# Expert-gate one-hots in 2-byte form, with the third part of the gate multiplied on ScalarE

## The chip, the cores and the metric

The kernel runs on one core of a Trainium2 chip. The metric is the device time of one execution in microseconds (us); lower is better. A core has TensorE (PE, matrix products; PEld is its weight load), VectorE (DVE), ScalarE (ACT), GpSimd (POOL) and SyncE (SP, which here only issues transfers). Each of these works through its own queue in the order of the program and waits on semaphores for the others.

## The reference, cut to what matters

One transformer layer on 512 tokens of width 1024: a token mixer (differential attention and a spatial gating branch), then a channel mixer that retrieves single-neuron experts by product keys. The change touches only the second part:

```python
def peer(h, w_query, sub_keys, u_tab, v_tab):
    q = rmsnorm((xt @ w_query).reshape(T, PEER_HEADS, 2, PEER_PK_DIM))
    s = jnp.einsum('thpd,pnd->thpn', q, sub_keys).astype(jnp.float32)
    s1, i1 = lax.top_k(s[:, :, 0], PEER_TOPK)
    s2, i2 = lax.top_k(s[:, :, 1], PEER_TOPK)
    cand = (s1[..., :, None] + s2[..., None, :]).reshape(T, PEER_HEADS, n_cand)
    cidx = (i1[..., :, None] * PEER_N_KEYS + i2[..., None, :]).reshape(T, PEER_HEADS, n_cand)
    best, pos = lax.top_k(cand, PEER_TOPK)
    eidx = jnp.take_along_axis(cidx, pos, axis=-1)
    gate = jax.nn.softmax(best, axis=-1)
    ...
        act = jax.nn.gelu(jnp.einsum('td,thkd->thk', xb, u_tab[ib]), approximate=False) * gb.astype(xb.dtype)
        return jnp.einsum('thk,thkd->td', act, v_tab[ib])
```

There are 8 heads, 16 picks a head (128 picks a token) and 128 x 128 = 16,384 experts; all data is fp32.

## The kernel before

Tokens come in four tiles of 128. For three of them (NB = 3, tiles 0 to 2) no expert is gathered. The kernel computes the activation of every expert for all 384 tokens, block by block (128 blocks of 128 experts), and multiplies it by a dense gate matrix that is zero except at a token's picks. The fourth tile (NA = 1) is done by gathering: 128 steps, each fetches one picked row of u and v for each token (1 MB, `fetch`, issued by POOL), takes the dot product on DVE (`dot`, tile `dj`), then GELU and the gate, and adds the scaled v row to `acc` on DVE (`accumulate`).

The stretches that matter here, in order:

1. Query products and scores (PE), with the first U blocks between them. A U block (`u_pass`, `next_u`) is 24 matrix products of 384 columns for 128 experts (three products, high and low halves, for each of 8 slices), then a GELU on ACT (tile `gS`) and a spill to DRAM (`gS_d`). The fp32 weights of a block are split by `w_split`: ACT writes `w_hi` (line 173) and DVE writes `w_lo` = raw minus `w_hi` (line 184). The split that a U block issues is that of the block two further on.
2. `merge` (lines 899 to 959), all on DVE but one exponential: the top 16 of the candidates of a head (`top16`, eight times a tile), the place of each pick in the two lists, and the two key numbers of each pick by a one-hot sum over 16 (tile `eq`, in fp32: compare, multiply, reduce, four halves a tile). It is a generator. `advance(x)` runs it piece by piece until the pieces' declared costs (the numbers that it yields) have used up x. Tiles 3 and 0 come before the gate loop, tiles 1 and 2 inside it.
3. The gate loop (from line 1115): 48 batches of 8 tokens. For each token the 128 x 128 gate matrix is a product over the 128 picks of two one-hot matrices: `oh_a` (which second key; on ACT as relu(1 - (iota - key)^2), two batches ahead) and `oh_b` (which first key, times the gate; on DVE, one batch ahead). `gate_matrix` multiplies them on PE in fp32 (line 1106, tile `ps_G`), ACT evicts to `stg` (line 1108), and every second batch 1 MB goes to `G_d`. After each batch stand one U block (`next_u`), a piece of `merge` (`advance(2.8)`) and, from batch 10, gather steps up to a planned share (`gather_to`; PICKS_G is the share that is due by batch 42).
4. U blocks that are left over, then the V stage: 128 blocks, each loads `gS` and, every eighth block, a slab `Gc` of the gate matrix, multiplies them (`at`), splits (`ah`, `al`) and accumulates 18 products of 512 columns in `po`. From block 74 a U block comes with each. PICKS_V is the share of gather steps between V blocks 4 and 74.

PE, DVE, ACT and POOL run in the order in which the code is written; only SP's transfers are ordered by the framework. At most three splits (`w_hi`, `w_lo`) are alive, and four raw blocks.

## Time and profile before

| | |
|---|---|
| device time, median of 3 runs | 2055.9 us (2055.06 to 2058.75) |
| the profiled execution, its own time | 2058.6 us |
| its span, first to last instruction | 2056.8 us |
| mean granted TensorE clock | 0.983 of full |
| busy: PE, DVE, ACT, POOL | 1929.4, 1607.0, 1008.4, 389.8 us |
| bytes moved, mean rate | 484.40 MB, 236 GB/s |

A busy sum over the whole span hides that the stages differ: in the V stage PE has no gap, in the gate loop all three of PE, DVE and ACT are busy for most of the time. So it is read by stretch, and in the gate loop by the start of each batch on PE.

### The profile page before, as it was taken

The numbers are of one execution on the slowest core, as the hardware profiler recorded it, in microseconds if no ns is written. First come the engines' busy times: TensorE is split into PE (matmuls) and PEld (weight loads), VectorE is DVE, ScalarE is ACT, GpSimd is POOL, SyncE is SP. The second block draws the span as 40 slices with busy tenths as digits, with TensorE's granted clock in tenths as the row PEclk, the third lists the DMA queues.
The fourth block names the chain that finished last, engine by engine and source line by source line (L and its number), as shares of the span: only waits on it lengthen the run. The fifth ranks groups of instructions, "written<-read, shape, count | busy, mean of one in ns | idle before, by whom it ended". The sixth has DMA issues, their size and how long they took to land.

```text
span 2056.8 us, 28318 instructions
## 1 busy us (share of the span) xinstructions
PE 1929.4 (94%) x10042; PEld 1693.9 (82%) x10042; DVE 1607.0 (78%) x3108; ACT 1008.4 (49%) x1947; POOL 389.8 (19%) x237
## 2 busy tenths in 40 slices
PE   6989999999989899789889999899999999999997
PEld 5768888887868798688888999688888899998996
DVE  7657877736775657999998785688888899899887
ACT  4235555544433455446889987333333333333333
POOL 0023232101000124330002110011112133333321
PEclk9999999999989999999999999999999999999999
DMA  8753323244875454346659999899998799989982
GB/s 320 276 165 88 94 77 103 79 158 125 277 237 200 137 158 154 120 164 207 190 182 322 306 320 294 302 320 335 324 332 315 273 346 353 341 324 344 347 313 96
DMA packets 171229, 484.40 MB, mean 236 GB/s; under 512 B 14384, under 2 KB 82896, under 8 KB 152528
## 3 DMA queue, kind: packets, MB, share of 16 engines
q1 hardware_dynamic: 152656, 348.37, 50.5%
q0 software_dynamic: 18432, 134.23, 17.8%
q8 instruction: 79, 1.29, 0.2%
q14 instruction: 62, 0.51, 0.1%
HBM read 424.72 MB, written 49.43 MB: 231 GB/s over the span
## 4 chain that ended last, share of the span: by engine, by line
PE 64%; DVE 18%; issue 8%; DMA 5%; ACT 4%; POOL 1%; SPq 0%; DVEq 0%; ACTq 0%; POOLq 0%
PE po L202 8%; PE po L203 8%; PE po L204 8%; PE ps_u L204 5%; PE ps_u L203 5%; PE ps_u L202 5%; DVE w_lo L184 2%; PE ps_proj L202 2%; PE ps_G L1106 2%; PE ps_proj L203 2%; PE ps_proj L204 2%; DMA w_raw<-in_wada 2%; PE ps_s L488 2%; ACT oh_a L1086 2%; PE ps_o L522 2%
## 5 line engine op out<-in xcount | busy, mean ns | idle before, releaser
L173 ACT ACTIVATE w_hi<-w_raw 128x1024 fp32r<-128x1024 f32 x370 | 391.1, 1058 | 466.8 <-issue 269.1
L184 DVE TENSOR_TENSOR w_lo<-w_raw,w_hi 128x1024 fp32r<-128x1024 f32 x330 | 404.6, 1227 | 170.9 <-ACT w_hi L173 166.1
L838 POOL DMA_INDIRECT uv<-in_uv,eidx x128 | 211.2, 1650 | 872.5 <-DVE acc L854 534.9
L204 PE MATMUL ps_u<-h2B,w_lo 128*128 128x384 f32 x1024 | 348.1, 340 | 18.7 <-DVE w_lo L184 18.7
L202 PE MATMUL ps_u<-h2B,w_hi 128*128 128x384 f32 x1024 | 351.9, 344 | 1.1 <-ACT h2B L770 1.1
L203 PE MATMUL ps_u<-h2B,w_hi 128*128 128x384 f32 x1024 | 347.0, 339 | 0.6 <-DVE r L84 0.6
L202 PE MATMUL po<-w_hi,ah 128*128 128x512 f32 x768 | 304.0, 396 | 7.7 <-ACT ah L1179 7.7
L204 PE MATMUL po<-w_hi,al 128*128 128x512 f32 x768 | 303.9, 396 | 0.0
L203 PE MATMUL po<-w_lo,ah 128*128 128x512 f32 x768 | 303.9, 396 | 0.0
L204 PEld LDWEIGHTS ps_u<-h2B,w_lo 128*128 128x128 f32 x1024 | 194.4, 190 | 21.3 <-DVE w_lo L184 21.3
L202 PEld LDWEIGHTS ps_u<-h2B,w_hi 128*128 128x128 f32 x1024 | 194.7, 190 | 4.3 <-ACT h2B L770 1.5
L203 PEld LDWEIGHTS ps_u<-h2B,w_hi 128*128 128x128 f32 x1024 | 194.4, 190 | 3.8 <-DVE r L84 1.0
L202 PEld LDWEIGHTS po<-w_hi,ah 128*128 128x128 f32 x768 | 144.5, 188 | 40.8 <-ACT ah L1179 8.0
L204 PEld LDWEIGHTS po<-w_hi,al 128*128 128x128 f32 x768 | 144.4, 188 | 35.2
L203 PEld LDWEIGHTS po<-w_lo,ah 128*128 128x128 f32 x768 | 144.4, 188 | 33.0 <-DVE w_lo L184 0.4
L854 DVE SCALAR_TENSOR_TENSOR acc<-uv,act,acc 128x1024 f32<-128x1024 f32 x127 | 163.2, 1285 | 4.5
L845 DVE SCALAR_TENSOR_TENSOR dj<-uv,h2A 128x1024 bf16<-128x1024 f32 x128 | 156.0, 1219 | 0.9
L184 POOL TENSOR_TENSOR w_lo<-w_raw,w_hi 128x1024 fp32r<-128x1024 f32 x40 | 97.3, 2436 | 249.9 <-ACT w_hi L173 245.9
L1177 DVE TENSOR_TENSOR at<-gS,Gc 128x384 f32<-128x384 f32 x128 | 121.2, 947 | 12.3 <-DMA gS<-gS_d 12.3
L1179 ACT ACTIVATE ah<-at 128x384 fp32r<-128x384 f32 x128 | 66.4, 518 | 125.4 <-DVE at L1177 125.1
L812 ACT ACTIVATE gS<-ps_u 128x384 f32<-128x384 f32 x128 | 62.7, 490 | 131.5 <-PE ps_u L204 130.9
L1106 PE MATMUL ps_G<-oh_b,oh_a 128*128 128x128 f32 x768 | 99.8, 283 | 26.2 <-DVE oh_b L1095 25.8
(307 smaller groups left out, 3495.2 us busy)
## 6 DMA issues: line engine op xcount, KB each, us to landing
w_raw<-in_uT SPq DMA_DIRECT2D x128, 512.0 KB, 5.7
w_raw<-in_uv SPq DMA_DIRECT2D x128, 512.0 KB, 6.5
w_raw<-in_w SPq DMA_DIRECT2D x120, 512.0 KB, 3.6
G_d<-stg SPq DMA_DIRECT2D x24, 1024.0 KB, 6.1
Gc<-G_d SPq DMA_DIRECT2D x16, 1536.0 KB, 9.7
ada_w<-in_wada SPq DMA_DIRECT2D x32, 512.0 KB, 10.0
w_raw<-in_wada SPq DMA_DIRECT2D x32, 512.0 KB, 4.4
gS_d<-gS SPq DMA_DIRECT2D x74, 192.0 KB, 3.9
```

The costliest lines, as they stand in the source:

```text
L173: nc.scalar.activation(hi, r, AF.Copy)
L184: eng.tensor_tensor(lo, r, hi.bitcast(F32), op=ALU.subtract)
L202: nc.tensor.matmul(ps, lh, rh, start=first, stop=False)
L203: nc.tensor.matmul(ps, lh, rl, start=False, stop=False)
L204: nc.tensor.matmul(ps, ll, rh, start=False, stop=last)
L812: nc.scalar.activation(g, ps, AF.Gelu)
L838: nc.gpsimd.indirect_dma_start(out=g, out_offset=None, in_=a["uv"], in_offset=bass.IndirectOffsetOnAxis(ap=eidx[:, t - NB, k:k + 1], axis=0))
L845: nc.vector.scalar_tensor_tensor(junk, g[:, :D], 1.0, h2A[t - NB], op0=ALU.mult, op1=ALU.mult, accum_out=act)
L854: nc.vector.scalar_tensor_tensor(acc[t - NB], g[:, D:], act, acc[t - NB], op0=ALU.mult, op1=ALU.add)
L1106: nc.tensor.matmul(pG[:, i], oa[:, q * 4 + i], ob[:, q * 4 + i], start=True, stop=True)
L1177: nc.vector.tensor_tensor(at, gS.pop(b), Gc[b // GCH][:, :, b % GCH], op=ALU.mult)
L1179: nc.scalar.activation(ah, at, AF.Copy)
```

## The change

Six things change together.

- The one-hot sums of `merge` work in 2-byte elements, on all eight heads at once, and the reduce is replaced by a tree of halving adds. The declared cost of a piece goes from 3.4 (four a tile) to 3.6 (two a tile).
- `oh_a` moves from ACT to DVE, as one 2-byte compare over eight tokens, and is made one batch ahead, not two.
- `oh_b` becomes three 2-byte matrices, one for each of three 2-byte parts of the gate. DVE makes the plain one-hot `oh_e` and the first two products; ACT makes the third (`last_part`, eight instructions, one a token, with the rest of the gate as a per-partition scale). `gate_matrix` sums three 2-byte products for each token in place of one fp32 product.
- The gather step's product by the gate moves from DVE to ACT (`gelus`), and GELU and gate of a step are issued ahead of the next `last_part`, so `accumulate` comes one round later.
- `advance(2.8)` in the gate loop becomes `advance(2.2)`.
- PICKS_G goes from 0.2 to 0.16, PICKS_V from 0.24 to 0.26, and RESERVE from 0 to 2 (the loop stops issuing U blocks when only so many are left).

```diff
@@ -823,15 +823,15 @@
...
-    PICKS_G, PICKS_V = 0.2, 0.24
-    RESERVE = 0
+    PICKS_G, PICKS_V = 0.16, 0.26
+    RESERVE = 2
...
-    coming, pend = [], []
+    coming, dots_, pend = [], [], []
...
@@ -845,22 +845,30 @@
...
+    def gelus():
+
+        while dots_:
+            t, k, g, act = dots_.pop(0)
+            nc.scalar.activation(act, act, AF.Gelu)
+            nc.scalar.activation(act, act, AF.Copy, scale=gate[:, t, k:k + 1])
+            pend.append((t, k, g, act))
+
     def accumulate(t, k, g, act):
-        nc.scalar.activation(act, act, AF.Gelu)
-        nc.vector.tensor_tensor(act, act, gate[:, t, k:k + 1], op=ALU.mult)
         if k == 0:
             nc.vector.tensor_scalar_mul(acc[t - NB], g[:, D:], act)
         else:
             nc.vector.scalar_tensor_tensor(acc[t - NB], g[:, D:], act, acc[t - NB], op0=ALU.mult, op1=ALU.add)
 
-    def gather_end(left=0):
-        while len(pend) > left:
+    def gather_end():
+        gelus()
+        while pend:
             accumulate(*pend.pop(0))
 
     def gather_step():
-        gather_end(1)
+        if len(dots_) + len(pend) > 1:
+            gather_end()
         if len(coming) == LEAD or (coming and not steps):
-            pend.append(dot(*coming.pop(0)))
+            dots_.append(dot(*coming.pop(0)))
         if steps:
             coming.append(fetch(*steps.pop(0)))
 
@@ -874,7 +882,8 @@
...
-        iota16 = iota[:, :TOPK]
+        iota16 = k1.tile([P, TOPK // 2, 2], BF16, name="iota16")
+        nc.vector.tensor_copy(iota16, iota[:, :TOPK].rearrange("p (a b) -> p a b", b=2))
...
@@ -933,20 +942,26 @@
...
-            idxf = k1.tile([P, 16, TOPK], F32, name="idxf")
-            nc.vector.tensor_copy(idxf, idx[t])
+            idxb = k1.tile([P, 16, TOPK], BF16, name="idxb")
+            nc.vector.tensor_copy(idxb, idx[t])
+            ij2 = k1.tile([P, 2, NH * TOPK, 2], BF16, name="ij2")
+            nc.vector.tensor_copy(ij2, ij.rearrange("p s h k -> p s (h k)").unsqueeze(3).to_broadcast([P, 2, NH * TOPK, 2]))
             yield 1.1
             nc.scalar.activation(g, g, AF.Exp)
             for p in range(2):
-                for hh in range(0, NH, 4):
-                    eq = pool.tile([P, 4, TOPK, TOPK], F32, name="eq", bufs=1)
-                    nc.vector.tensor_tensor(eq, ij[:, p, hh:hh + 4].unsqueeze(3).to_broadcast([P, 4, TOPK, TOPK]),
-                                            iota16.unsqueeze(1).unsqueeze(1).to_broadcast([P, 4, TOPK, TOPK]),
-                                            op=ALU.is_equal)
-                    iv = idxf.rearrange("p (h s) k -> p h s k", s=2)[:, hh:hh + 4, p]
-                    nc.vector.tensor_tensor(eq, eq, iv.unsqueeze(2).to_broadcast([P, 4, TOPK, TOPK]), op=ALU.mult)
-                    nc.vector.reduce_sum(ef[:, p, hh:hh + 4], eq, axis=AX.X)
-                    yield 3.4
+                eq = pool.tile([P, NH, TOPK, TOPK], BF16, name="eq", bufs=1)
+                shape = [P, NH * TOPK, TOPK // 2, 2]
+                nc.vector.tensor_tensor(eq.rearrange("p h k (a b) -> p (h k) a b", b=2),
+                                        ij2[:, p].unsqueeze(2).to_broadcast(shape),
+                                        iota16.unsqueeze(1).to_broadcast(shape), op=ALU.is_equal)
+                iv = idxb.rearrange("p (h s) k -> p h s k", s=2)[:, :, p]
+                nc.vector.tensor_tensor(eq, eq, iv.unsqueeze(2).to_broadcast([P, NH, TOPK, TOPK]), op=ALU.mult)
+                w = TOPK // 2
+                while w > 1:
+                    nc.vector.tensor_tensor(eq[:, :, :, :w], eq[:, :, :, :w], eq[:, :, :, w:2 * w], op=ALU.add)
+                    w //= 2
+                nc.vector.tensor_tensor(ef[:, p], eq[:, :, :, 0], eq[:, :, :, 1], op=ALU.add)
+                yield 3.6
                 if p == 0:
                     z = sm.tile([P, NH], F32, name="gz")
                     nc.vector.reduce_sum(z, g, axis=AX.X)
@@ -1060,7 +1075,9 @@
 
         with tc.tile_pool(name="pg", bufs=3, space=PSUM) as pgp, tc.tile_pool(name="k2", bufs=2, side="right") as k2:
             stg = {}
-
+            PAIR = [P, 8, P // 2, 2]
+            iota2 = k2.tile([P, P // 2, 2], BF16, name="iota2", bufs=1)
+            nc.vector.tensor_copy(iota2, iota.rearrange("p (a b) -> p a b", b=2))
             pks, oas, obs = {}, {}, {}
 
             def picks_of(t):
@@ -1073,37 +1090,53 @@
                     for k in range(2):
                         nc.tensor.transpose(pt[:, k], ef[:, k].rearrange("p h k -> p (h k)"), ident)
                     nc.tensor.transpose(pt[:, 2], gate[:, t], ident)
-                    pks[t] = k2.tile([P, 3, P], F32, name="pk")
-                    nc.scalar.activation(pks[t], pt, AF.Copy)
+                    pk = k2.tile([P, 4, P, 2], BF16, name="pk")
+                    nc.scalar.activation(pk[:, 0:3], pt.unsqueeze(3).to_broadcast([P, 3, P, 2]), AF.Copy)
+                    g3 = k2.tile([P, P], F32, name="g_rest")
+                    nc.vector.tensor_tensor(g3, pt[:, 2], pk[:, 2, :, 0], op=ALU.subtract)
+                    nc.vector.tensor_copy(pk[:, 3], g3.unsqueeze(2).to_broadcast([P, P, 2]))
+                    nc.vector.tensor_tensor(g3, g3, pk[:, 3, :, 0], op=ALU.subtract)
+                    pks[t] = pk, g3
                 return pks[t]
 
+            def per_token(pk, k, o):
+                return pk[:, k, o * 8:o * 8 + 8].unsqueeze(2).to_broadcast(PAIR)
+
+            def pairs(x):
+                return x.rearrange("p t (a b) -> p t a b", b=2)
+
             def one_hots_a(t, o):
 
-                pk = picks_of(t)
-                oa = oas[t, o] = k2.tile([P, 8, P], F32, name="oh_a", bufs=3)
+                oa = oas[t, o] = k2.tile([P, 8, P], BF16, name="oh_a")
+                nc.vector.tensor_tensor(pairs(oa), iota2.unsqueeze(1).to_broadcast(PAIR), per_token(picks_of(t)[0], 1, o),
+                                        op=ALU.is_equal)
+
+            def one_hots_b(t, o):
+
+                pk = picks_of(t)[0]
+                eq = k2.tile([P, 8, P], BF16, name="oh_e")
+                nc.vector.tensor_tensor(pairs(eq), iota2.unsqueeze(1).to_broadcast(PAIR), per_token(pk, 0, o),
+                                        op=ALU.is_equal)
+                ob = k2.tile([P, 3, 8, P], BF16, name="oh_b")
+                obs[t, o] = ob, eq
+                for k in range(2):
+                    nc.vector.tensor_tensor(pairs(ob[:, k]), pairs(eq), per_token(pk, 2 + k, o), op=ALU.mult)
+
+            def last_part(t, o):
+                ob, eq = obs[t, o]
                 for i in range(8):
-                    k = o * 8 + i
-                    nc.scalar.activation(oa[:, i], iota, AF.Square, scale=-1.0, bias=pk[:, 1, k:k + 1])
-                nc.scalar.activation(oa, oa, AF.Relu, scale=-1.0, bias=ones[:, 0:1])
-
-            def one_hots_b(t, o):
-
-                t0 = o * 8
-                pk = picks_of(t)
-                ob = obs[t, o] = k2.tile([P, 8, P], F32, name="oh_b")
-                for i in range(8):
-                    nc.vector.tensor_scalar(ob[:, i], iota, pk[:, 0, t0 + i:t0 + i + 1], pk[:, 2, t0 + i:t0 + i + 1],
-                                            op0=ALU.is_equal, op1=ALU.mult)
+                    nc.scalar.activation(ob[:, 2, i], eq[:, i], AF.Copy, scale=picks_of(t)[1][:, o * 8 + i:o * 8 + i + 1])
 
             def gate_matrix(t, o):
 
-                oa, ob = oas.pop((t, o)), obs.pop((t, o))
+                oa, (ob, _) = oas.pop((t, o)), obs.pop((t, o))
...
                 for q in range(2):
                     pG = pgp.tile([P, 4, P], F32, name="ps_G")
                     for i in range(4):
-                        nc.tensor.matmul(pG[:, i], oa[:, q * 4 + i], ob[:, q * 4 + i], start=True, stop=True)
+                        for k in range(3):
+                            nc.tensor.matmul(pG[:, i], oa[:, q * 4 + i], ob[:, k, q * 4 + i], start=k == 0, stop=k == 2)
...
@@ -1119,19 +1152,21 @@
             for _ in range(UA):
                 next_u()
             one_hots_a(*batches[0])
+            one_hots_b(*batches[0])
+            last_part(*batches[0])
             for _ in range(UB):
                 next_u()
-            one_hots_a(*batches[1])
-            one_hots_b(*batches[0])
             for i, (t, o) in enumerate(batches):
                 if i + 1 < len(batches):
+                    one_hots_a(*batches[i + 1])
                     one_hots_b(*batches[i + 1])
                 gate_matrix(t, o)
+                gelus()
+                if i + 1 < len(batches):
+                    last_part(*batches[i + 1])
                 if nu[0] < n_ahead - RESERVE:
                     next_u()
-                if i + 2 < len(batches):
-                    one_hots_a(*batches[i + 2])
-                advance(2.8)
+                advance(2.2)
                 gather_end()
                 if i >= G_FROM:
                     gather_to(PICKS_G * (i + 1 - G_FROM) / (G_TO - G_FROM) if i < G_TO else 0)
@@ -1208,6 +1243,7 @@
             else:
                 v_w = w_get("v", b)
             ah, al = parts
+            gelus()
             nxt = None
             if b + 1 < NBLK:
                 if (b + 1) % GCH == 0:
```

ACT's queue through one batch with a gather step and on to the next batch's one-hots, before and then changed. `stg` is the eviction of a batch, `act` the GELU (and gate) of a gather step, `w_hi` the split of the U block two further on, `gS` the GELU of the current U block.

```order
L1108 ACTIVATE stg_10406<-ps_G_10480 128x4x16x8
L1108 ACTIVATE stg_10406<-ps_G_10486 128x4x16x8
L173 ACTIVATE w_hi_10495<-w_raw_10419 128x1024
L812 ACTIVATE gS_10524<-ps_u_10499 128x384
L1086 ACTIVATE oh_a_10527<-iota_5718,pk_9435 128x128 x8
L1087 ACTIVATE oh_a_10527<-oh_a_10527,ones_77 128x1024
L849 ACTIVATE act_10466<-act_10466 128x1
```

```order
L1141 ACTIVATE stg_10680<-ps_G_10766 128x4x16x8
L1141 ACTIVATE stg_10680<-ps_G_10780 128x4x16x8
L852 ACTIVATE act_10754<-act_10754 128x1
L853 ACTIVATE act_10754<-act_10754,gate_5333 128x1
L1128 ACTIVATE oh_b_10763<-oh_e_10761,g_rest_9592 128x128 x8
L173 ACTIVATE w_hi_10807<-w_raw_10719 128x1024
```

The split `w_hi` stood directly behind the eviction; now the eight instructions of the third gate part stand ahead of it, and they read `oh_e`, which DVE writes.

DVE's queue over the same piece of the program, before and then changed. `acc` and `dj` are the accumulation and the dot product of the gather steps.

```order
L1095 TENSOR_SCALAR oh_b_10471<-iota_5718,pk_9435 128x128 x8
L184 TENSOR_TENSOR w_lo_10496<-w_raw_10419,w_hi_10495 128x1024
L850 TENSOR_TENSOR act_10466<-act_10466,gate_5333 128x1
L854 SCALAR_TENSOR_TENSOR acc0_5712<-uv_10247,act_10466,acc0_5712 128x1024
L1095 TENSOR_SCALAR oh_b_10540<-iota_5718,pk_9435 128x128 x8
```

```order
L1118 TENSOR_TENSOR oh_e_10675<-iota2_7932,pk_9590 128x1024
L1123 TENSOR_TENSOR oh_b_10677<-oh_e_10675,pk_9590 128x1024 x2
L184 TENSOR_TENSOR w_lo_10722<-w_raw_10634,w_hi_10721 128x1024
L860 SCALAR_TENSOR_TENSOR acc0_5712<-uv_10257,act_10668,acc0_5712 128x1024
L845 SCALAR_TENSOR_TENSOR dj_10755,act_10754<-uv_10421,h2A0_5331 128x1024
L1111 TENSOR_TENSOR oh_a_10759<-iota2_7932,pk_9590 128x1024
L1118 TENSOR_TENSOR oh_e_10761<-iota2_7932,pk_9590 128x1024
L1123 TENSOR_TENSOR oh_b_10763<-oh_e_10761,pk_9590 128x1024 x2
```

Between one `oh_e` and the next stands `w_lo`, which reads the `w_hi` that ACT now writes behind its third part; the gather step's two instructions stand between `w_lo` and the next `oh_e`, and its multiplication by the gate is gone from here.

SP's queue from the last write of the gate matrix to the first loads of the V stage, before and then changed (`gS_d` writes are the spills of U blocks).

```order
L1112 DMA G_d_85<-stg_11691 128x16x128
L160 DMA w_raw_11877<-in_uv 128x1024
L1173 DMA Gc_11867<-G_d_85 128x3072
L160 DMA w_raw_11909<-in_uv 128x1024
L160 DMA w_raw_11941<-in_uv 128x1024
L821 DMA gS_11863<-gS_d_84 128x384
```

```order
L1145 DMA G_d_85<-stg_12169 128x16x128
L814 DMA gS_d_84<-gS_12300 128x384
L160 DMA w_raw_12369<-in_uv 128x1024
L1208 DMA Gc_12419<-G_d_85 128x3072
L160 DMA w_raw_12429<-in_uv 128x1024
L160 DMA w_raw_12461<-in_uv 128x1024
L821 DMA gS_12415<-gS_d_84 128x384
```

One more U block's spill now stands behind the last write of the gate matrix: four U blocks are left there, against three. The order on every engine is the same with RESERVE at 0 as at 2; the fourth block is there because the cheaper declared pieces of `merge` end the wait for tile 0 one U block earlier.

## Rows read from the trace of the kernel before

**Rows 1.** Busy time by stretch: us, busy of PE, PEld, DVE, ACT, POOL (instructions), clock, DMA.

```profile
800.00:954.00 154.00, 129.56 (x692) 118.06 (x691) 143.97 (x531) 72.97 (x164) 53.00 (x26) 0.97 0.47 161
954.00:1273.00 319.00, 293.38 (x1905) 286.08 (x1906) 268.86 (x707) 285.80 (x644) 33.38 (x23) 1.00 0.80 259
1273.00:1293.00 20.00, 12.27 (x72) 11.95 (x70) 4.60 (x5) 5.30 (x9) 0.00 (x0) 0.93 0.96 326
1293.00:2045.00 752.00, 751.98 (x3528) 646.17 (x3528) 652.04 (x862) 278.66 (x472) 175.52 (x104) 1.00 0.86 313
```

**Rows 2.** Order of time on PE: first, second-last and last gate batch, one U start.

```profile
954.43 2.19 PE L1106 MATMUL ps_G<-oh_b,oh_a 128*128 128x128 f32 x16 [1.05 <-DVE oh_b L1095]
...
1264.80 1.95 PE L1106 MATMUL ps_G<-oh_b,oh_a 128*128 128x128 f32 x16
...
1266.50 0.42 PE L202 MATMUL ps_u<-h2B,w_hi 128*128 128x384 f32 x1
...
1270.77 1.95 PE L1106 MATMUL ps_G<-oh_b,oh_a 128*128 128x128 f32 x16
```

**Rows 3.** Who waited for whom in the gate loop (945 to 1290): us, times, longest.

```profile
DVE act L850 <- ACT act L849: 27.9, 17, 3.5
...
PE ps_G L1106 <- DVE oh_b L1095: 25.8, 23, 2.0
```

**Rows 4.** Order of time on ACT through one batch: start, us, line, instruction.

```profile
1186.82 0.49 ACT L812 ACTIVATE gS<-ps_u 128x384 f32<-128x384 f32 x1 [1.64 <-PE ps_u L204]
1187.21 2.44 ACT L1086 ACTIVATE oh_a<-iota,pk 128x128 f32<-128x128 f32 x8
...
1190.83 1.06 ACT L1108 ACTIVATE stg<-ps_G 128x512 f32<-128x512 f32 x2
1191.79 1.05 ACT L173 ACTIVATE w_hi<-w_raw 128x1024 fp32r<-128x1024 f32 x1
```

**Rows 5.** Order of time on DVE through the gather step of that batch.

```profile
1191.15 1.28 DVE L854 SCALAR_TENSOR_TENSOR acc<-uv,act,acc 128x1024 f32<-128x1024 f32 x1
1192.35 1.22 DVE L845 SCALAR_TENSOR_TENSOR dj<-uv,h2A 128x1024 bf16<-128x1024 f32 x1
...
1193.49 2.13 DVE L1095 TENSOR_SCALAR oh_b<-iota,pk 128x128 f32<-128x128 f32 x8
```

**Rows 6.** The chain of waits in a batch with three top-16 pieces of merge.

```profile
1014.83 2.04 DVE oh_b L1095 x8
1016.87 1.13 DVE w_lo L184
1022.07 2.04 DVE oh_b L1095 x8
```

**Rows 7.** Order of time on DVE: one half-size one-hot sum and the start of the next.

```profile
928.74 1.22 DVE L943 TENSOR_TENSOR eq<-ij,iota 128x1024 f32<-128x1024 f32 x1
...
932.50 1.23 DVE L943 TENSOR_TENSOR eq<-ij,iota 128x1024 f32<-128x1024 f32 x1
```

**Rows 8.** DVE operations by shape: busy us, mean ns, idle before (third row: 954 to 1067).

```profile
L184 DVE TENSOR_TENSOR w_lo<-w_raw,w_hi 128x1024 fp32r<-128x1024 f32 x330 | 404.6, 1227 | 170.9 <-ACT w_hi L173 166.1 <-DMA wsT<-in_wsT 4.2
...
L278 DVE TENSOR_TENSOR rb<-rb,sq 128x512 f32<-128x512 f32 x7 | 4.8, 692 | 6.7 <-ACT sq L277 6.0
...
L905 DVE TENSOR_TENSOR val<-val,rq 128x256 f32<-128x256 f32 x1 | 0.4, 415 | 0.0
...
L934 DVE TENSOR_TENSOR ij<-ij,t 128x128 f32<-128x128 f32 x4 | 1.2, 292 | 0.1
```

**Rows 9.** Order of time on PE: 256-column products, one weight load each.

```profile
145.22 0.28 PE L203 MATMUL ps_proj<-hcT,w_hi 128*128 128x256 f32 x1
145.34 0.28 PE L204 MATMUL ps_proj<-hcT,w_lo 128*128 128x256 f32 x1
```

**Rows 10.** Who waited for whom ahead of the gate loop (800 to 950).

```profile
PE ps_u L204 <- DVE w_lo L184: 18.7, 8, 6.1
```

**Rows 11.** The chain of waits from the U blocks into the V stage.

```profile
1284.19 7.14 DMA gS<-gS_d
```

## Prediction

> **What bounds the kernel now.** I read the stretches first. In the V stage PE is busy for 751.98 of 752 us, so nothing that the change does to DVE or ACT can shorten it, and a gather step moved into it is hidden there. The room is ahead of it: in the gate loop PE, DVE and ACT are busy for 293, 269 and 286 of 319 us, all three close to the limit; ahead of the loop DVE is (144 of 154); and 7.7 us of PE are idle on the way into the V stage [rows 1]. Then I read the starts of the gate batches on PE. From the first to the last it is 316.3 us for 47 intervals, 6.73 us each, while an undisturbed interval takes 5.97: 1.70 for the gate product and 4.27 for the U block [rows 2]. So 47 x 5.97 = 280.6 us is PE at its pace and 35.7 us is waiting. The waits name the two causes: PE waits for `oh_b` (25.8 us in 23 times), and DVE, which makes it, waits for the GELU of a gather step (27.9 us in 17 times) that stands on ACT behind `oh_a` [rows 3, 4].
>
> **The gate product on PE.** 16 half products of fp32 become 24 products of 2-byte elements with a weight load each. No row shows a 2-byte product. The nearest is the 256-column product: 0.12 us each with its own weight load, 0.107 of it the columns at the 2.4 GHz level, so 0.013 over [rows 9]. For 128 columns that gives 0.053 + 0.013 = 0.067 us, or 1.61 us a batch against 1.70: PE's own pace goes from 5.97 to 5.88, 47 x 0.09 = 4 us. The bounds are 0.053 (columns alone) and 0.107 (no faster than the 1.70 / 16 of an fp32 half): a pace of 5.5 to 6.8. I take 0.067. The Trainium skill speaks against even that little: its page "TensorE: Matmul & The Clock Gate", section "Back-to-back issue gap", puts a stream of weight-load and product pairs at 128 columns at about 81 ns, by which 24 would take an estimated 1.94 us, more than the fp32 product, and PE's pace would be 6.2. As the next part shows, PE is not what sets the pace, so the sum moves by 2 to 3 us between the one and the other.
>
> **The new loop through DVE and ACT.** This is where I expect the time to go. The order shows four steps that wait for one another inside one batch. ACT's third part of the next batch reads `oh_e` of DVE. The split `w_hi` stands on ACT behind that third part (before it stood ahead of the one-hots). DVE's `w_lo` reads `w_hi`. And the next `oh_a` and `oh_e` stand on DVE behind `w_lo` and behind whatever `merge` and gather work has been put between. So each batch must pay for all of it in a row:
> third part: eight ACT instructions of 128 elements with a per-partition operand, as `oh_a` had, 2.44 us less the 0.10 by which ACT overlaps neighbours = 2.34 [rows 4]; `w_hi` 1.05 [rows 4]; `w_lo` 1.13 [rows 6]; `oh_a` and `oh_e`; hand-offs, 0.1 in all.
> The two compares are 2-byte operations of 1024 elements, of which the trace has none. Their ends are 1.23 us, an fp32 operation of 1024 elements at one a cycle, and 0.69, one of 512, if pairs go through together [rows 8]. I take 0.69, because both inputs and the output are laid out in pairs of neighbours and every operand is 2-byte: 0.60 + 0.69 = 1.29 (the first overlaps by 0.09, as `w_lo` does). The Trainium skill's page "VectorE: DVE Perf Modes", section "The perf-mode tier table", gives a two-tensor operation on 2-byte SBUF operands twice the fp32 rate, which is the end that I took; no row here can show it, and at the other end the sum would be 2170 instead of 2096 (below).
> The loop is 2.34 + 1.05 + 1.13 + 1.29 + 0.10 = 5.91 us, just above PE's 5.88, and 47 x 5.91 = 277.8. In itself that is no loss. The loss is that DVE's other work is no longer beside it. DVE has only the first two gate products (1.2 us) to do during the third part and the split (3.39 us), then sits idle for some 2.1 us, and everything else stands between `w_lo` and the next `oh_e` and adds to the interval in full:
> - 13 top-16 searches of `merge` in the loop (three are done ahead of it): three take 7.24 - 2.04 - 1.13 = 4.07 [rows 6], so 13 x 1.36 = 17.6.
> - Four one-hot sums of eight heads: 1.23 + 1.23 + 0.69 + 0.42 + 0.3 + 0.3 by fp32 rows of half as many elements [rows 7, 8], with hand-offs 4.3, against 2 x 3.76 before [rows 7]: 17.2 (at one a cycle 7.2 each, 29).
> - Thirty short instructions of about 0.29 [rows 8] and one tile's candidate adds: 10.
> - 18 dots and 18 accumulations of gather steps (20 steps are started in the loop against 26): 18 x (1.20 + 1.14) [rows 5] = 42.1.
> - Two changes of tile, with three more small DVE instructions behind the transposes: 2.
> Together 277.8 + 17.6 + 17.2 + 10 + 42.1 + 2 = 366.7 against 316.3: **+50.4 us**. The wait of 27.9 us for the GELU is gone indeed (GELU and gate stand ahead of the third part now), and so is the DVE multiplication; what comes in its place costs more. PE then idles up to 4 us in the batches with merge work; should its clock drop there, the U block still ends before the next third part does.
>
> **Ahead of the loop.** Tiles 3 and 0 are merged there: four sums at 7.52 - 4.3 = 3.2 less, minus two copies that make the pairs, is 12 us less DVE work in a stretch in which DVE is busy for 94% and PE waits 18.7 us for `w_lo` [rows 1, 10]. One U block (4.27) also leaves this stretch. The first batch comes between 4.3 us (the U block alone) and 16 us (both) earlier; I take 12, since much of PE's wait there is that DVE work. The U block comes back behind the last batch, +4.3: net **-7.7** (0 to -12).
>
> **Into the V stage.** PE idles 7.7 us there, while the load of `gS`, issued when the second-last U block frees its raw block, takes 7.14 us at a DMA share of 0.96 [rows 1, 11]. One more U block ahead of it lets the slab `Gc` land earlier, so the load competes with less, but its issue is still tied to the U blocks: **-2.5** (0 to -7.7). RESERVE does nothing: the loop never comes down to two blocks. The V stage itself: two gather steps more before block 74 at a DMA share of 0.86, no waiting PE: 0.
>
> **Sum.** The profiled execution took 2058.6 us: 2058.6 + 50.4 - 7.7 - 2.5 = 2098.8. It lies 2.7 us above the median of the runs, so I forecast **2096 us** as the median, slower by 40.
>
> **Rivals.** (1) Faster: DVE and ACT are not tied. It needs a `w_hi` that is ready when DVE comes to `w_lo`, which is so when third part and split take no more than the 1.2 us of the two gate products beside them; at the rows' prices they take 3.39. If they did, DVE would set the pace in the ten batches with merge work (10 x 3.5 + 45 = 80) and PE in the other 37 (218): 298 in place of 316.3, and with the other terms 2056 - 18 - 10 = 2027. For it speaks that the loop before ran with all three engines near their limits and that both named waits vanish; against it the order. 0.12. (2) DVE takes one 2-byte element a cycle: 47 x 1.06 + 4 x 2.9 in the loop and 12 us of the gain ahead of it lost: 2096 + 74 = 2170. For it speaks that the operands repeat rows and elements; 0.06. (3) Weight loads hold the product at 0.107 us: PE's pace is 6.84, which binds only in the eight or so batches without merge or gather work: +7 us, inside my range. (4) The tie is real but part of the gather and merge work slips into DVE's idle time: 2050 to 2070; 0.07.
>
> **Numbers.** My own case, 0.75, spans 2070 to 2118 (loop at 5.75 a batch, all terms at their good ends; or the stretch ahead of the loop giving nothing, with (3)). The range of 8 in 10 is 2060 to 2125; it leaves out (1), (2) and the lower part of (4). About 0.2% (4 us) is what a measurement of this kernel can tell from no change. Slower by more: 0.84; within: 0.03; faster: 0.13.
>
> **What would show it.** Right: batch starts on PE of about 5.9 us in the last batches, 7 to 8.3 with gather steps and 9 to 10 with three searches or a sum; DVE idle in front of `w_lo`, released by `w_hi`, some 2 us a batch and near 100 us in all; `ps_G` released by ACT; `oh_a` at 0.7 us; the V stage still without a gap. Wrong: a loop of 300 us or less with `w_lo` not waiting (then rival 1), or `oh_a` at 1.2 us (rival 2).

## The result, and the profile after

The changed kernel takes **2110.8 us** (median of 4 runs, 2109.4 to 2111.9) against 2056.9 for the kernel before, measured beside it: a ratio of 1.026 (95% interval 1.025 to 1.027). It is slower by 54 us, where 40 was forecast. Its profiled execution took 2111.8 us, with a span of 2109.6.

The view of busy time by stretch, with the stretches cut at the first and last gate batch and at the first product of the V stage (columns as in [rows 1]):

```profile
800.00:954.00 154.00, 132.38 (x678) 120.90 (x676) 140.00 (x574) 68.90 (x159) 53.68 (x27) 0.92 0.47 158
954.00:1320.00 366.00, 295.31 (x2263) 277.55 (x2262) 260.68 (x457) 238.83 (x609) 24.30 (x18) 0.93 0.68 211
1320.00:1345.00 25.00, 18.61 (x122) 18.16 (x122) 7.59 (x8) 10.43 (x20) 0.00 (x0) 0.98 0.86 283
1345.00:2098.00 753.00, 752.89 (x3528) 646.64 (x3528) 650.52 (x772) 307.59 (x587) 175.91 (x109) 1.00 0.88 321
```

The V stage still has no gap, and the stretch ahead of the gate loop is as long as it was. In the loop, 366 us now, PE has the busy time of before, and DVE and ACT have less than before (261 and 239 us, against 269 and 286 in [rows 1]). Each is busy for a smaller share of it, and the loop has become longer. That is how a chain of engines that wait for one another looks.

The starts of the first and last gate batch on PE, in order of time; they answer to [rows 2]:

```profile
954.02 0.23 PE L1139 MATMUL ps_G<-oh_b,oh_a 128*128 128x128 bf16 x1
...
1320.01 0.23 PE L1139 MATMUL ps_G<-oh_b,oh_a 128*128 128x128 bf16 x1
```

The loop's 47 intervals take 366.0 us against 316.3. So the difference of 52.8 us between the two spans is divided as follows: up to the first gate batch -0.4, the loop +49.7, from the last gate batch to the first V product +2.6 (22.2 us before, 24.8 after), the rest +1.0.

The waits of DVE, ACT and PE inside the loop (954 to 1320); they answer to [rows 3]:

```profile
DVE w_lo L184 <- ACT w_hi L173: 101.3, 47, 2.2
...
ACT oh_b L1128 <- DVE oh_e L1118: 99.7, 47, 5.6
ACT act L852 <- DVE dj L845: 26.8, 18, 2.3
...
PE ps_G L1139 <- DVE oh_b L1123: 70.5, 72, 5.7
```

DVE waits for ACT once in each of the 47 intervals, and ACT waits for DVE once in each: they take turns. PE waits for DVE's two gate products, up to twice a batch. The start of a longer batch shows it, on DVE, ACT and PE:

```profile
969.09 1.29 DVE L1123 TENSOR_TENSOR oh_b<-oh_e,pk 128x1024 bf16<-128x1024 bf16 x2
969.14 2.44 ACT L1128 ACTIVATE oh_b<-oh_e,g_rest 128x128 bf16<-128x128 bf16 x8 [5.27 <-DVE oh_e L1118]
969.83 0.29 PE L1139 MATMUL ps_G<-oh_b,oh_a 128*128 128x128 bf16 x1 [3.68 <-DVE oh_b L1123]
970.43 2.61 PE L1139 MATMUL ps_G<-oh_b,oh_a 128*128 128x128 bf16 x23 [0.31 <-DVE oh_b L1123]
972.80 0.67 PE L202 MATMUL ps_u<-h2B,w_hi 128*128 128x384 f32 x1
```

All 72 waits of PE end 0.05 to 0.06 us after a gate product of DVE; ACT's third part has begun before that and does not hold PE up. So the third part costs its time not at PE but in the turns of ACT and DVE. The 27.9 us that DVE waited for the GELU of a gather step are gone, as was intended; in its place ACT waits for the dot product (26.8 us), within its turn.

One turn without merge or gather work, first on DVE, then on ACT, in order of time (start, us):

```profile
1072.65 1.22 DVE L184 TENSOR_TENSOR w_lo<-w_raw,w_hi 128x1024 fp32r<-128x1024 f32 x1 [2.19 <-ACT w_hi L173]
1073.79 0.69 DVE L1111 TENSOR_TENSOR oh_a<-iota,pk 128x1024 bf16<-128x1024 bf16 x1
1074.39 0.68 DVE L1118 TENSOR_TENSOR oh_e<-iota,pk 128x1024 bf16<-128x1024 bf16 x1
1075.11 1.29 DVE L1123 TENSOR_TENSOR oh_b<-oh_e,pk 128x1024 bf16<-128x1024 bf16 x2
1078.60 1.22 DVE L184 TENSOR_TENSOR w_lo<-w_raw,w_hi 128x1024 fp32r<-128x1024 f32 x1 [2.20 <-ACT w_hi L173]
```

```profile
1075.17 2.45 ACT L1128 ACTIVATE oh_b<-oh_e,g_rest 128x128 bf16<-128x128 bf16 x8 [1.22 <-DVE oh_e L1118]
1077.53 1.04 ACT L173 ACTIVATE w_hi<-w_raw 128x1024 fp32r<-128x1024 f32 x1
```

From one `w_lo` to the next it is 5.95 us. Within them `w_lo` ends at 1073.87, `oh_e` at 1075.07, the third part at 1077.62 and `w_hi` at 1078.57; then `w_lo` can start. All that DVE has to do meanwhile is the 1.3 us of the first two gate products.

### The profile page after: what moved, and what is told of

Read it like the earlier page. It is cut to its first block, busy times and chain, and to the rows that moved or that the text cites. A ratio compares the mean times of both kernels' runs of the same rounds, so it can differ in the third digit from the quotient of the medians.

```text
span 2109.6 us, 28649 instructions
## 1 busy us (share of the span) xinstructions
PE 1939.3 (92%) x10426; PEld 1693.4 (80%) x10426; DVE 1594.5 (76%) x2803; ACT 989.7 (47%) x2027; POOL 380.4 (18%) x237
## 4 chain that ended last, share of the span: by engine, by line
PE 55%; DVE 19%; ACT 9%; issue 6%; DMA 4%; POOL 1%; ACTq 0%; POOLq 0%; DVEq 0%
PE po L204 8%; PE po L202 8%; PE po L203 8%; ACT oh_b L1128 5%; PE ps_u L203 4%; PE ps_u L204 4%; PE ps_u L202 4%; DVE w_lo L184 4%; ACT w_hi L173 2%; PE ps_proj L202 2%; DMA w_raw<-in_wada 2%; PE ps_proj L203 2%; PE ps_proj L204 2%; PE ps_s L488 2%; PE ps_o L522 1%
## 5 line engine op out<-in xcount | busy, mean ns | idle before, releaser
L838 POOL DMA_INDIRECT uv<-in_uv,eidx x128 | 201.4, 1573 | 925.8 <-DVE acc L860 745.1
L204 PE MATMUL ps_u<-h2B,w_lo 128*128 128x384 f32 x1024 | 352.6, 344 | 12.6 <-DVE w_lo L184 12.6
L202 PE MATMUL ps_u<-h2B,w_hi 128*128 128x384 f32 x1024 | 359.2, 351 | 1.1 <-ACT h2B L770 1.1
L203 PE MATMUL ps_u<-h2B,w_hi 128*128 128x384 f32 x1024 | 352.3, 344 | 0.6 <-DVE r L84 0.6
L202 PEld LDWEIGHTS ps_u<-h2B,w_hi 128*128 128x128 f32 x1024 | 200.0, 195 | 4.1 <-ACT h2B L770 1.4
L203 PEld LDWEIGHTS ps_u<-h2B,w_hi 128*128 128x128 f32 x1024 | 199.5, 195 | 3.8 <-DVE r L84 1.0
L1128 ACT ACTIVATE oh_b<-oh_e,g_rest 128x128 bf16<-128x128 bf16 x384 | 117.5, 388 | 102.8 <-DVE oh_e L1118 102.8
L1139 PE MATMUL ps_G<-oh_b,oh_a 128*128 128x128 bf16 x1152 | 90.2, 236 | 70.9 <-DVE oh_b L1123 70.7
L1139 PEld LDWEIGHTS <-oh_a 128*128 128x128 bf16 x1152 | 75.9, 106 | 88.9 <-DVE oh_b L1123 69.2
```

Source lines behind the costliest of these rows:

```text
L202: nc.tensor.matmul(ps, lh, rh, start=first, stop=False)
L203: nc.tensor.matmul(ps, lh, rl, start=False, stop=False)
L204: nc.tensor.matmul(ps, ll, rh, start=False, stop=last)
L838: nc.gpsimd.indirect_dma_start(out=g, out_offset=None, in_=a["uv"], in_offset=bass.IndirectOffsetOnAxis(ap=eidx[:, t - NB, k:k + 1], axis=0))
L1128: nc.scalar.activation(ob[:, 2, i], eq[:, i], AF.Copy, scale=picks_of(t)[1][:, o * 8 + i:o * 8 + i + 1])
L1139: nc.tensor.matmul(pG[:, i], oa[:, q * 4 + i], ob[:, k, q * 4 + i], start=k == 0, stop=k == 2)
```

## Experiments

All times below are medians; the ratio is to runs of the kernel before on the same chip, with its 95% interval. The loop is the time from the first to the last gate batch in the profile of the run.

**split_first** puts the split ahead of the third part on ACT and changes nothing else.

```diff
...
                 gate_matrix(t, o)
                 gelus()
+                u_w = w_get("u", nu[0])
                 if i + 1 < len(batches):
                     last_part(*batches[i + 1])
-                if nu[0] < n_ahead - RESERVE:
-                    next_u()
+                next_u(u_w)
...
```

(`w_get` hands out the weights of the block and issues the split of the one two further on. The condition with RESERVE falls away; it never held a U block back.)

> The changed kernel with one change of order on ScalarE: the split w_hi of the U block two further on is issued ahead of the eight instructions of the third gate part instead of behind them. No work is added or removed. Theory (the loop is tied: oh_e on VectorE, third part, w_hi, w_lo, oh_e in a row): w_lo no longer waits for the third part, so a batch takes the longer of PE's pace (5.6 us in the trace of the changed kernel) and VectorE's own work (3.73 us plus its merge or gather work): about 10 x 7.9 + 18 x 6.1 + 19 x 5.6 = 295 us against 366 for the loop, so about 2040 us (2030 to 2055). Rival (VectorE simply has more work in the loop, or ScalarE is the bound, whatever the order): within 5 us of 2111.

Measured: **2035.1 us**, ratio 0.991 (0.988 to 0.994), the loop 290.1 us. The same instructions in another order on one engine are worth 76 us. DVE's wait in the loop, and then ACT's order of time through one interval:

```profile
DVE w_lo L184 <- ACT w_hi L173: 21.4, 18, 2.1
```

```profile
1091.57 1.27 ACT L1141 ACTIVATE stg<-ps_G 128x512 f32<-128x512 f32 x2 [0.19 <-PE ps_G L1139]
1092.74 0.19 ACT L852 ACTIVATE act<-act 128x1 f32<-128x1 f32 x1
1092.96 0.29 ACT L853 ACTIVATE act<-act,gate 128x1 f32<-128x1 f32 x1
1093.17 1.04 ACT L173 ACTIVATE w_hi<-w_raw 128x1024 fp32r<-128x1024 f32 x1
1094.11 2.44 ACT L1128 ACTIVATE oh_b<-oh_e,g_rest 128x128 bf16<-128x128 bf16 x8
1096.47 0.49 ACT L812 ACTIVATE gS<-ps_u 128x384 f32<-128x384 f32 x1
```

DVE's busy time in the loop is 260.6 us, as in the changed kernel (260.7): not the amount of work, but the order cost the time. The third part now runs while DVE writes `w_lo`. ACT waits for PE again (0.19 us in front of `stg`), and 33 of the 47 intervals are PE's pace, 5.6 us; those with a gather step are no longer than the rest. The other rival, that ACT or DVE has simply too much to do, is out.

**split_gate** puts the split ahead of the evictions as well (`u_w = w_get(...)` stands in front of `gate_matrix`).

> The changed kernel with the split w_hi issued still earlier on ScalarE: ahead of the two evictions of the gate product, so that it does not wait for the gate product either. Theory (the tie is the third part ahead of the split): most of the gain is there already with the split behind the evictions, so within 4 us of the run split_first, about 2038 us. Rival (what counts is that the split stands behind the eviction, which waits for the gate product): this run is faster than split_first by 10 us or more. Second rival (amount of work): 2111.

Measured: 2036.9 us, ratio 0.990 (0.988 to 0.992), the loop 291.3 us. So that the split stands behind the evictions costs nothing; it was the third part alone.

**no_third** leaves the third part out.

```diff
...
-                        for k in range(3):
+                        for k in range(2):
...
-                if i + 1 < len(batches):
-                    last_part(*batches[i + 1])
...
```

> The changed kernel without the third gate part (the eight instructions of ScalarE and the eight products of a batch that use it are left out, so the gate is summed from two parts only). Theory (the third part's 2.34 us stand in the tie of every batch): the tie is gone, pace of PE 16 products and the U block, about 5.15 us: 10 x 7.9 + 18 x 6.1 + 19 x 5.15 = 287 us for the loop, 2031 us in all (2020 to 2050). Rival (the third part is hidden on ScalarE): only PE's eight products are saved, 47 x 8 x 0.06 = 23 us, 2088.

Measured: 2019.7 us, ratio 0.981 (0.980 to 0.983), the loop 273.1 us, 93 less than in the changed kernel; DVE waits for `w_hi` for 7.7 us in 5 times. The rival's 23 us are out. Compared with split_first, where the third part is there but out of the chain, it saves 17 us, about what PE's eight products take (33 intervals of 5.14 in place of 5.59 are 15 us).

**third_dve** makes the third part on DVE, with one more 2-byte multiplication.

```diff
...
-                for k in range(2):
+                for k in range(3):
                     nc.vector.tensor_tensor(pairs(ob[:, k]), pairs(eq), per_token(pk, 2 + k, o), op=ALU.mult)
...
```

> The changed kernel with the third gate part made on VectorE, as one more 2-byte multiplication of 1024 elements, in place of eight instructions on ScalarE. VectorE gets 0.6 us more work a batch. Theory (the tie through ScalarE costs, not VectorE's amount of work): the loop takes about 10 x 8.5 + 18 x 6.7 + 19 x 5.6 = 311 us, 2056 us in all (2045 to 2070). Rival (VectorE's amount of work sets the loop): 47 x 0.6 = 28 us slower than the changed kernel, 2139.

Measured: 2047.7 us, ratio 0.995 (0.993 to 0.997), the loop 301.5 us. More work on DVE, and 63 us less time: DVE waits for `w_hi` in 5 intervals, 5.8 us in all. These four runs settle the loop.

**stop0** and **exp_late** ask why the first gate batch did not come 12 us earlier. In stop0 the wait for tile 0 ends as soon as tile 0 is merged, so the searches of tile 1 that the changed kernel runs there go into the loop.

```diff
...
-            while us > 0 and any(todo):
+            while us > 0 and any(todo) and stop not in done:
...
-                advance(4.0)
+                advance(4.0, 0)
...
```

> The changed kernel, but the wait for tile 0 ahead of the gate loop stops when tile 0 is merged: the candidate adds and three top-16 searches of tile 1, which the changed kernel runs ahead of the loop (943.10 to 948.81 us), go into the loop. Theory (these searches took back part of the gain ahead of the loop, and in the tied loop VectorE's work is paid in full): first gate batch about 4 to 5 us earlier (949 to 950 in place of 954.0), the loop 4 to 5 us longer, total unchanged at 2111 (2107 to 2115). Rival (the first batch is held by PE's U blocks at the low clock, not by VectorE): first batch still at 953 to 954, total 2115.

Measured: 2115.5 us, ratio 1.028 (1.026 to 1.030), first gate batch at 952.8, the loop 371.6 us. The theory failed ahead of the loop: without the searches the first batch came only 1.2 us earlier, and in this execution the first score product, long before them, already came 1.2 us earlier (733.8 us against 735.0). In the loop it held: searches and candidate adds made it 5.6 us longer, their full price, as the tie says.

The next view is ACT's order of time in the changed kernel, then the row of PE that waits for it:

```profile
895.26 1.28 ACT L950 ACT_TABLE_LOAD   x1
906.11 0.31 ACT L950 ACTIVATE gate<-gate 128x128 f32<-128x128 f32 x1 [9.57 <-DVE gate L929]
906.33 1.04 ACT L173 ACTIVATE w_hi<-w_raw 128x1024 fp32r<-128x1024 f32 x1
907.39 1.28 ACT L812 ACT_TABLE_LOAD   x1
908.68 0.49 ACT L812 ACTIVATE gS<-ps_u 128x384 f32<-128x384 f32 x1
```

```profile
909.71 1.11 PE L1039 MATMUL ps_qT<-ident,qn 128*128 128x128 f32 x4 [4.97 <-ACT qn L1070]
```

The cheaper declared costs of `merge` bring tile 0's exponential forward, on ACT ahead of the eviction `qn` of the last query product. There it waits 9.57 us for DVE, and `qn`, the transposes and the last scores wait behind it. In the kernel before it stood behind the last scores, with nothing to wait for:

```profile
928.01 0.31 ACT L939 ACTIVATE gate<-gate 128x128 f32<-128x128 f32 x1
```

So exp_late issues the exponential after the first one-hot sum:

```diff
...
-            nc.scalar.activation(g, g, AF.Exp)
             for p in range(2):
...
                 if p == 0:
+                    nc.scalar.activation(g, g, AF.Exp)
+                    yield 0.3
                     z = sm.tile([P, NH], F32, name="gz")
...
```

> The changed kernel with the exponential of a tile's gate issued on ScalarE behind the first one-hot sum instead of ahead of it (the sum does not need it). Theory (the cheaper declared costs of merge pull tile 0's exponential, on ScalarE, ahead of the eviction of qn; there it waits 9.6 us for VectorE, and PE waits 4.97 us for qn behind it, so the first gate batch does not come earlier): that wait of PE for qn goes below 2 us and the first gate batch comes at 948 to 950 in place of 954.0, as it did in the run before_merge by less work; the loop stays at 366: about 2106 us (2102 to 2109). Rival (PE at its low clock holds the first batch): first batch still at 953 to 954, 2111.

Measured: 2110.6 us, ratio 1.025 (1.024 to 1.027): the first gate batch is at 948.8, where it was expected, and PE's wait is 1.07 us, but the total is the same as without it, within the spread of the runs, and not the 2106 of the theory. Of the 5.3 us by which the first gate batch is earlier, 2.4 are there already at the first score product. The loop is 367.9 us, 1.9 longer, and the rest behind the last gate batch 1.5 longer. Most of the 1.9 stands in the two intervals in which the exponentials of tiles 1 and 2 come now; each is 0.86 us longer, and DVE waits there for the exponential:

```profile
DVE gz L968 <- ACT gate L965: 1.5, 2, 0.8
```

The 1.5 us behind the loop have no cause that these runs show. Since executions differ by some us ahead of the change already, I also read this from the first to the last score product, in the tile view of `ps_sc` (the kernel before, the changed one, exp_late):

```profile
L1015 PE MATMUL ps_sc<-keysT,qT x128: 272/275/276, 733.0 to 917.6; 128*128 128x128 f32 x128
```

```profile
L1030 PE MATMUL ps_sc<-keysT,qT x128: 270/275/275, 735.0 to 922.5; 128*128 128x128 f32 x128
```

```profile
L1031 PE MATMUL ps_sc<-keysT,qT x128: 270/275/275, 732.6 to 917.3; 128*128 128x128 f32 x128
```

That is 184.6, 187.5 and 184.7 us. In the profiles of all runs that have the early exponential it is 187.5 to 190.6; in the two without the new sums and the three with the late exponential it is 184.5 to 184.7. So the early exponential costs 3 to 6 us there. From the last score product to the first gate batch it is 36.9 us before and 31.5 in the changed kernel and in exp_late: 5.4 less, of which 4.3 are the U block that left this stretch. That DVE has 12 us less to do there is worth about 1 us: in the changed kernel PE runs its U blocks one behind the other from 922.5 on, with 3.7 us of waits in all.

**before_merge** and **before_gelu** take one part of the change each to the kernel before: the 2-byte one-hot sums with their declared costs, and GELU and gate on ACT ahead of the split.

> The kernel before with one part of the change: the one-hot sums of merge in 2-byte form, with the new declared costs (which bring the three searches of tile 1 ahead of the loop as well). Theory (the sums are cheaper by 3.0 us each, four ahead of the loop less 4.1 us of searches, four in it): first gate batch at about 947 in place of 954.4, the loop 5 to 10 us shorter, one U block (4.2 us) more behind it: about 2047 us (2040 to 2053). Rival (VectorE's work is not on the path ahead of the loop): first batch at 953 to 954, total 2052 to 2057.

Measured: 2061.8 us (median of 10 runs, 2056.4 to 2067.1), ratio 1.002 (1.001 to 1.004). The first gate batch is at 948.1, but the profile of this run is 5.2 us ahead of the kernel before already at the first score product, so only 1.2 us of that are left to the change; the loop is 1.7 us shorter, and the U block comes back behind it. (The profiled execution is the fastest of the ten, 2056.4 us.) The early exponential is there too (it waits 10.0 us), so what the sums would bring without it stays open. The theory failed: the cheaper sums with their declared costs bring nothing here.

> The kernel before with one part of the change: GELU and gate of a gather step are both on ScalarE and are issued right behind the eviction of the gate product, ahead of w_hi and oh_a, instead of behind oh_a; nothing else is changed. Theory (this part is sound, and the loss comes from the third part alone): VectorE's wait of 27.9 us for the GELU goes, a batch with a gather step falls from 7.36 us to ScalarE's own pace of about 6.3 (1.06 + 0.5 + 1.05 + 0.4 + 3.3), 18 batches by 1.05: 19 us, about 2039 us (2030 to 2050). Rival (the wait only moves: the GELU now stands ahead of w_hi and waits there for the dot product on VectorE, so w_lo and the U blocks wait): 2053 to 2062, or slower.

Measured: **2042.3 us**, ratio 0.993 (0.992 to 0.995), the loop 301.5 us. The intervals with a gather step fell from 7.36 to 6.0 to 6.3 us, and what DVE still waits for in the loop is `w_hi` (34.2 us in 31 times). This part of the change is sound by itself: 15 us.

**sf_adv1**, **sf_adv1_stop**, **best1** and **best4** build on split_first. There the first twelve intervals, those with merge work, are 6.1 to 9.7 us. All four spread `merge` more thinly.

```diff
...
-                advance(2.2)
+                advance(1.0)
...
```

> The run split_first with merge spread more thinly: advance(1.0) in place of advance(2.2) in the gate loop, so one top-16 search a batch in place of three. Theory (in the first twelve batches of split_first, 7.5 to 9.7 us each, VectorE's work of three searches on top of its own 3.73 us sets the pace): with one search VectorE needs 5.1 us, less than PE's 5.59, so nearly all batches run at 5.59: the loop takes 270 to 275 us against 290, total about 2017 us (2010 to 2025). Rival (the first twelve batches are held by the order of w_hi or by the low clock): within 5 us of 2035.

Measured: 2030.1 us, ratio 0.987 (0.985 to 0.988), the loop 282.0 us. Half right: seven of the first nine intervals are at PE's pace, but one whole one-hot sum on DVE still makes an interval of 8.8 us, and two that meet gather steps there make 10.7 and 10.3, with 7.7 behind them.

> The run sf_adv1 with the searches of tile 1 moved from ahead of the loop into it, as in stop0. Theory (in the loop without the tie VectorE has room for them): first gate batch about 4 us earlier and the loop no longer than in sf_adv1, about 2013 us. Rival (no room, or the first batch is held by PE): equal to sf_adv1 within 2 us.

Measured: 2029.1 us, ratio 0.986 (0.984 to 0.987), first gate batch at 954.2, the loop 288.1 us in its profiled execution, which took 2035.5: nothing gained, which agrees with stop0.

best1 cuts each sum in three pieces and has the late exponential:

> The run sf_adv1 with two more changes: the late exponential of exp_late, and each one-hot sum cut into three pieces of declared cost 1.2, so that a gate batch has at most some 2 us of merge work instead of 4.5. Theory (what is left in sf_adv1 above PE's 5.59 us a batch are the batches in which a whole sum meets a gather step on VectorE: 8.8, 10.7, 10.3, 7.7 us): nearly all intervals at 5.59, the loop 266 to 273 us against 282; with a first batch 4 us earlier about 2014 us (2008 to 2022). Rival (the excess of those batches is the exponential on ScalarE or the change of tile): the loop stays at 280, total 2025 to 2030.

Measured: 2028.7 us, ratio 0.985 (0.984 to 0.987), the loop 289.1 us. The theory's condition was not met: with one piece a batch the merge of a tile ends just where its picks are needed, and the intervals at the two changes of tile are 9.0, 7.2 and 10.2, 9.9, 7.2 us. So best4 runs up to two pieces a batch, makes the picks one batch earlier, and has the exponential behind the multiplication of the first sum:

```diff
...
-                advance(2.2)
+                advance(1.2)
...
+                if i + 2 < len(batches):
+                    picks_of(batches[i + 2][0])
...
```

> The run split_first with merge spread evenly: advance(1.2), each one-hot sum in three pieces of declared cost 1.2, the exponential between the multiplication and the adds of the first sum, and the transposed picks of the next tile made one batch earlier. In best1 merge was spread so thinly that the sums of a tile were only just done at the change of tile (intervals of 9.0, 7.2 and 10.2, 9.9, 7.2 us there). Theory (only VectorE's pile-up in single batches is left above 5.59): the loop takes 268 to 276 us against 289 in best1 and 290 in split_first, about 2017 us (2010 to 2024). Rival (the gather steps' share of VectorE holds the loop at 282 to 290 however merge is spread): 2026 to 2035.

Measured: **2017.6 us**, ratio 0.981 (0.980 to 0.983): faster than both kernels, by 40 and 93 us. The loop by stretch (columns as in [rows 1]):

```profile
946.73:1226.71 279.98, 268.09 (x2263) 256.74 (x2263) 261.12 (x474) 244.10 (x615) 26.12 (x18) 1.00 0.88 277
```

The work is that of the changed kernel, done in 280.0 us with PE busy for 268 and a mean granted clock of 1.00. The loop is 4 us above the range that I expected: gather steps and merge still meet in nine intervals of 6.1 to 7.7 us, and seven at the start, without gather steps, are 6.1 to 6.5.

## Why the prediction was right, and where it was off

*The loop* was forecast at 366.7 us and is 366.0. A turn was put at 5.91 us and is 5.95; DVE's idle time at some 2.1 us a batch and near 100 us in all, and it is 101.3 us in 47 times. The other DVE work adds to the turn in full: intervals with both instructions of a gather step are 8.23 (5.95 + 2.34 = 8.29), those with three searches 10.0 (5.95 + 3 x 1.36 = 10.03); nothing of it slips into DVE's idle time, so rival 4 is out. One sign failed: `ps_G` was to be released by ACT, and DVE's gate products release it in all 72 waits. That leaves the tie as it is, since PE is no part of it. The runs split_first, no_third and third_dve show the cause: take the third part from in front of `w_hi`, by order, by leaving it out or by moving it, and 64 to 93 us of the loop go.

*Two bytes on DVE.* The compare of 1024 elements takes 0.685 us, the end that I took, with repeated rows as operands too; rival 2 is out. The rule of the Trainium skill, "VectorE: DVE Perf Modes", section "The perf-mode tier table", by which two-tensor operations on 2-byte SBUF operands run at twice the fp32 rate, agrees with 0.685 against the 1.22 of an fp32 operation [rows 8].

*PE's pace* was mis-sized: 5.59 us, not 5.88. In a batch without a wait the 24 products take 1.32 us (1076.93 to 1078.25), 55 ns each, close to my lower bound of 0.053 and not to the 0.067 that I took:

```profile
1076.93 1.51 PE L1139 MATMUL ps_G<-oh_b,oh_a 128*128 128x128 bf16 x24
1078.25 0.42 PE L202 MATMUL ps_u<-h2B,w_hi 128*128 128x384 f32 x1
```

Rival 3 is out. That nothing came of the error is luck: the tie was above both. The 81 ns of the Trainium skill, "TensorE: Matmul & The Clock Gate", section "Back-to-back issue gap", is not seen here; the same section's formula for an isolated product, N / 2.4 + 2.5 ns, gives 56 and agrees with the 55.

*The one-hot sums* were put at 4.3 us and take 4.5 (937.45 to the next instruction at 941.97): +0.9 in all for four.

*Rival 1*, that DVE and ACT are not tied, was priced at 2027 us. It is what split_first makes of the kernel, by an order that I had not looked for: 2035.

*Ahead of the loop* is the step that failed. I took 12 us, "since much of PE's wait there is that DVE work", and got 0.4 (2.4, measured from the first score product on). Two things were wrong in it. I had read off the order that three searches of tile 1 come ahead of the loop, and subtracted them in the loop, but not added them here; stop0 shows, however, that they weigh at most 1.2 us there. And I had not asked where the cheaper declared costs put tile 0's exponential on ACT, though an order shows it: exp_late puts that at 2.8 us, the other profiles with it at up to 6. Between the two profiles the 0.4 is made up of a first score product 2.0 us later, which is not the change, 2.9 more up to the last score product and 5.4 less from there to the first gate batch. The rest of the 12 was not on PE's path: the U block and about 1 us are all that this last stretch gave. This step alone is 11.6 of the 12.6 us by which the sum (+40.2) lay below the difference of the spans (+52.8).

*Into the V stage.* PE's idle time in front of the first V product went from 7.7 to 6.2 us: -1.5, where I took -2.5; with the U block +2.6 in place of +1.8.

*The clock.* I said that a lower clock in the merge batches would not show. It did fall (0.84 on average from 960 to 1064 us, against 1.00 between 1071 and 1088), and PE still waited 1.6 to 5.7 us (I had said up to 4) for DVE's first gate product at nine of the ten batch starts in that stretch: even at the lower clock it was early.

## What to carry to other kernels

Moving work to an engine that has room can lengthen a loop if the work stands in its queue ahead of something that another engine waits for: follow each moved instruction round, from engine to engine, and see whether the path closes on itself. When it does, every other instruction on that path is paid in full, as the searches and gather steps were here, and a change of order with the same instructions can undo it (here one line, 76 us). A change to the declared costs of a planner moves everything that it plans, so look on every engine at what now stands ahead of what.

## What was not expected of the hardware

- The stream of 128-column 2-byte products, each with its own weight load, runs at 55 ns a product, and in eight tied batches with merge work, where PE had idled 2.1 to 5.7 us before, 23 of them take 2.1 to 2.6 us in place of 1.4, and the first U product behind them up to 0.67 us in place of 0.42: PE is at the 1.2 GHz level there (granted clock 0.50 from 969 to 973), and back at the 2.4 GHz level within the U block (granted clock 0.84 over the stretch).
- An exponential between GELUs costs ACT two table loads of 1.28 us each. What they cost by themselves no run shows; the place of the exponential in the queue cost 3 to 6 us ahead of the loop.
- Executions differ by up to 8 us ahead of the changed code (first score product at 727.8 to 735.9 us in 14 profiles), so moves of a few us there can only be read from one event to the next within a profile, not from the span.
